# A written list of places for the weight splits of an encoder trunk, in place of a model of time

## The chip, the core and the metric

The kernel runs on one core of a Trainium2 chip. Its engines are TensorE (PE in the profile: matmuls, with PEld for its weight loads), VectorE (DVE), ScalarE (ACT), GpSimd (POOL) and SyncE (SP, which here only issues DMAs). Each has a queue of its own and works through it in order; between queues, semaphores hold an instruction back until what it needs is there. The metric is the time of one execution on the device in microseconds (us), as the median of several runs.

## The reference

The program is an encoder of two layers over a sequence of 256 tokens of width 1024, in float32. Each layer is a feed-forward block (SwiGLU), a mixer, and a second feed-forward block, each with a residual and a layer norm behind it. The mixer of the first layer is a bidirectional chunkwise mLSTM, that of the second a windowed attention with grouped heads.

```python
for l in range(DEPTH):
    x = layer_norm(ALPHA * x + 0.5 * swiglu(x, ffn_w_in[l, 0], ffn_w_out[l, 0]), ln_g[l, 0], ln_b[l, 0])
    j = l // N_MIXERS
    if l % N_MIXERS == 0:
        y = mlstm_mixer(x, ml_w_in[j], ml_gate_b[j], ml_norm_g[j], ml_w_out[j])
    else:
        y = window_attention(x, at_w_in[j], at_sink[j], at_w_out[j])
    x = layer_norm(ALPHA * x + y, ln_g[l, 1], ln_b[l, 1])
    x = layer_norm(ALPHA * x + 0.5 * swiglu(x, ffn_w_in[l, 1], ffn_w_out[l, 1]), ln_g[l, 2], ln_b[l, 2])

def swiglu(x, w_in, w_out):
    gu = x @ w_in
    g, u = gu[..., :D_FF], gu[..., D_FF:]
    return (jax.nn.silu(g) * u) @ w_out
```

With D_FF = 2816 the four feed-forward blocks hold nearly all of the weights and of the multiplications.

## The kernel before, in words

**Tiles and stages.** All 256 tokens stay on the chip: x as two tiles of 128 tokens, its transpose xT, and the hidden h. The weights stream through. There are six stages in a row, two FFN blocks around the mLSTM, then two around the attention. An FFN stage has two wide units of 512 columns and then three groups; a group is a unit of 256 columns (`beside`) and one of 512 (`seven`), the latter with seven products of half-size blocks in place of eight, for which sums of weight blocks are built beforehand. The second weight matrix is multiplied in as soon as its part of h is there (`down`), and six last rows of it in `tail`, with the layer norm (`Norm`) behind.

**Splits.** Every float32 factor is cut in two parts whose sum it is, a rounded one (`_hi`, float32r) and the rest (`_lo`), and every product is three matmuls (`mm3`: hi by hi, hi by lo, lo by hi). For a piece of weights, 128 by 1024, `Weights.high` writes w_hi on ACT, `Weights.low` writes w_lo on DVE. There are 388 pieces, in the order in which PE uses them (the plan). Weight sums for `seven` are done by `Weights.sum`, either on DVE (s_raw added to s_raw, 72 of them) or by an accumulating DMA issued on POOL (24). The same two engines also move every PSUM result out and split it (`split_evac`: h_hi and h_lo, xT_hi and xT_lo, ...), compute the activations, the products of gate and value, and the layer norms.

**Buffers and loads.** Raw weights are loaded into 4 buffers (w_raw), inside an FFN stage also into 6 (s_raw) and 2 more (v_raw). When the last split or sum of a raw tile is placed, `drop` frees it and `load` puts the next DMA on SP's queue; it waits there for the semaphores of the freed buffer. Split parts live in a ring of 10 pairs; `done` tells that PE has been given its last use of a pair, and raises `room`, up to which the splits may go ahead.

**What sets the order.** The order of instructions on each queue is the order in which the program calls them. For all but splits and sums it is written out in the stages. Splits and sums are slipped in between them:

- Inside an FFN stage by a model of time (`Paced`, L48): while the program is written, it adds up for each engine when an instruction would end (`on_vector`, `on_scalar`, `on_tensor`), marks for each tile when it would be there, and after every matmul calls `fill` (L266), which places a split or a sum when its engine would otherwise be no more than 300 ns ahead of PE.
- In the mixers and at the seams by counts: every `W.done(upto, most)` (L295) places up to so many splits there, the counts in lists written by hand (PU, TD, MP, PD at L29 to L36).
- `take` calls `split`, which places whatever the next pieces still lack.

Every engine call goes through `Engine.call` in L134, so that most instructions of the profile stand at that line, and are told apart by their tiles. An accumulating sum is issued at L263, loads at L98 and L100, the layer norm's g and b at L517.

Of the kernel before, what the change touches and what calls it, by code (L numbers as in the profile page):

```python
# [1 line left out]

# [26 lines left out]
PU = [3, 1, 2, 1, 1, 1, 1, 1, 0, 1, 1, 2]  # L29
# [4 lines left out]
TD = [0, 3, 2, 0, 2, 2]  # L34
MP = [1, 0, 0, 0, 1, 0, 1, 1, 0, 0, 0, 0, 2, 2, 2]
PD = [8, 0, 5, 9, 6]  # L36
# [3 lines left out]
AHEAD = 300.0  # L40
SOON = -1000.0
LANDING = 2200.0
LOADING = 1340.0
SECOND = 1250.0
ADDING = 8000.0


class Paced:  # L48

    def __init__(self, nc):
        self.nc = nc
        self.pe = self.vec = self.act = self.dma = 0.0
        self.there, self.places = {}, {}
        self.filler, self.alone = None, True
        self.vector = Engine(nc.vector, self.on_vector)
        self.scalar = Engine(nc.scalar, self.on_scalar)
        self.tensor = Engine(nc.tensor, self.on_tensor)
# [3 lines left out]

    def place(self, ap):

        f = ap.ap[0][0]
        key = (ap.offset % f if f else 0, tuple(ap.ap[1:]))
        if key not in self.places:
            i = np.array([key[0]])
            for step, n in key[1]:  # L70
                i = (i[:, None] + step * np.arange(n if step else 1)[None, :]).reshape(-1)
            self.places[key] = i
        return self.places[key]

    def when(self, *aps):
        t = 0.0
        for ap in aps:
            a = self.there.get(ap.name)
            if a is not None:
                i = self.place(ap)  # L80
                t = max(t, a[i[i < a.size]].max(initial=0.0))
        return t

    def mark(self, ap, t):
        i = self.place(ap)
        a = self.there.get(ap.name)
        if a is None or a.size <= i.max():
            self.there[ap.name] = np.zeros(int(i.max()) + 1)
            if a is not None:
                self.there[ap.name][:a.size] = a  # L90
        self.there[ap.name][i] = t

    def load(self, ap, source, engine=None):
        if engine is not None:
            engine.dma_start(ap, source)
        elif isinstance(source, list):
            for k, src in enumerate(source):
                self.nc.sync.dma_start(ap[:, k].rearrange("p (m f) -> p m f", m=src.shape[1]), src)  # L98
        else:
            self.nc.sync.dma_start(ap, source)  # L100
        come = self.pe + LANDING
        alone, self.alone = self.alone, come > self.dma
        self.dma = max(self.dma, come) + LOADING + (SECOND if alone and not self.alone else 0.0)
        self.mark(ap, self.dma)

    def on_vector(self, name, n, out, ins):
        self.vec = max(self.vec, self.when(*ins)) + (n + 71) / 0.96
        for o in out:
            self.mark(o, self.vec + 115)

    def on_scalar(self, name, n, out, ins):
        self.act = max(self.act, self.when(*ins)) + n * 0.912 + 25
        for o in out:
            self.mark(o, self.act + 125)

    def on_tensor(self, name, n, out, ins):
        self.pe = max(self.pe, self.when(*ins)) + (109.0 if name == "transpose" else n / 2.4 + 13.3)
        for o in out:
            self.mark(o, self.pe + 200)
        if self.filler is not None:  # L120
            self.filler()


class Engine:
    def __init__(self, engine, told):
        self.engine, self.told = engine, told

    def __getattr__(self, name):
        f = getattr(self.engine, name)
        if name.startswith("preload"):  # L130
            return f

        def call(out, *args, **kw):
            r = f(out, *args, **kw)  # L134
            ins = [x for x in [*args, *kw.values()] if hasattr(x, "ap")]
            outs = [out] + ([kw["accum_out"]] if "accum_out" in kw else [])
            size = lambda x: int(np.prod(x.shape[1:]))
            self.told(name, size(out) if name in ("matmul", "transpose") else max(map(size, [out] + ins)), outs, ins)
            return r
        return call  # L140


class Weights:
# [5 lines left out]
    def __init__(self, nc, pool, words, plan, after):  # L149
        self.nc, self.pool, self.words, self.plan, self.after = nc, pool, words, plan, after  # L150
        self.raw, self.parts, self.half, self.sums = {}, {}, [], []
# [4 lines left out]
        self.uses = [0] * len(words)  # L156
        for p in plan:
            self.uses[p["word"]] += 1
# [45 lines left out]
    def split(self, upto):  # L204
        while self.made < min(upto, len(self.plan)):
            self.high()
        while self.half and self.half[0][0] < upto:
            self.low()

    def high(self):  # L210

        nc, i = self.nc, self.made
        p = self.plan[i]
        while self.half and (p["word"] not in self.raw or any(h[0] == p["needs"] for h in self.half)):
            self.low()
        while any(s_[0] == p["needs"] or p["word"] not in self.raw for s_ in self.sums):
            self.sum()
        if p["word"] not in self.raw:
            return False
# [12 lines left out]
        return True  # L232

    def low(self):

        nc = self.nc
# [13 lines left out]
        self.sums += [(i, *sum_) for sum_ in self.after.get(i, ())]  # L250
# [3 lines left out]
    def sum(self):  # L254
        nc = self.nc
        _, w, v = self.sums.pop(0)
# [5 lines left out]
        else:  # L262
            nc.gpsimd.dma_start(t.rearrange("p (k f) -> p k f", k=self.words[w]["k"]), v, accum_op=OP.add)  # L263
            nc.mark(t, max(nc.vec, nc.pe) + ADDING)

    def fill(self):  # L266

        nc = self.nc
        while True:
            act, vec = max(nc.act, nc.pe), max(nc.vec, nc.pe)  # L270
            if act < nc.pe + AHEAD and len(self.half) < 2 and self.made < min(self.room, len(self.plan)):
                p = self.plan[self.made]
                if (p["word"] in self.raw and nc.when(self.raw[p["word"]]) < act + SOON
                        and not any(p["needs"] == x for x in [h[0] for h in self.half] + [s_[0] for s_ in self.sums])):
                    self.high()
                    continue
            if vec < nc.pe + AHEAD:
                if self.half and nc.when(self.half[0][1]) < vec + SOON:
                    self.low()
                    continue  # L280
                if self.sums and nc.when(*(self.raw[w] for w in self.sums[0][1:] if isinstance(w, int))) < vec + SOON:
                    self.sum()
                    continue
            break

    def take(self, n):
        i = self.used
        self.used += n
        self.split(self.used)
# [5 lines left out]
    def done(self, upto=None, most=None, high_only=False):  # L295

# [1065 lines left out]
```

## Time and profile before

| what | value |
|---|---|
| median of 3 runs | 942.11 us |
| lowest and highest | 941.06 and 942.29 us |
| span of the profiled execution | 941.2 us |
| PE busy | 925.3 us, 98% of the span, 4416 matmuls |
| DVE busy | 800.0 us, 85%, 943 instructions |
| ACT busy | 546.5 us, 58%, 781 |
| POOL busy | 103.2 us, 11%, 162 |
| from HBM | 185.68 MB, 198 GB/s over the span |

The span is that of one execution taken with the profiler, from its first instruction to its last; that execution was not one of the three that were timed, and of its time only the span is given. A row of the profile names line, engine, operation, the tile written and the tiles read (`w_lo<-w_raw,w_hi`); in the order of time a row has start and duration in us, and in brackets how long the engine had been idle before it and what ended that wait. A row "x2" holds two such instructions in a run.

### The profile page before, as it was taken

Reading aid. Unit: us, or ns where it says so; the run is one execution under the profiler, and the core shown is the slowest. Engines: PE = TensorE matmul, PEld = TensorE weight load, DVE = VectorE, ACT = ScalarE, POOL = GpSimd, SP = SyncE. Lnnn points to the kernel's source line nnn. Section 1 sums busy time; section 2 is a strip of 40 time slices with the busy share of each in tenths; the row PEclk is TensorE's granted clock in tenths of the full one; section 3 lists DMA queues with packets and bytes.
Section 4 is the critical chain, followed back from the end, with each engine's and each line's share of the span. In section 5 each row is a group of like instructions: output and inputs, shape, how many; then the busy total and the mean of one; then the engine's idle time right before and its main releaser. Section 6 shows DMA issues by size and latency. Waiting matters only on the chain.

```text
span 941.2 us, 12338 instructions
## 1 busy us (share of the span) xinstructions
PE 925.3 (98%) x4416; PEld 766.4 (81%) x4416; DVE 800.0 (85%) x943; ACT 546.5 (58%) x781; POOL 103.2 (11%) x162
## 2 busy tenths in 40 slices
PE   9999999999999999999999999999999999999996
PEld 7788888889878787888888888887887788888885
DVE  6899997787697889988888899977878888898975
ACT  5656756347563548565535566563678554757460
POOL 0030101011111000101010101010544300000100
PEclk9999999999999999999999999999999999999999
DMA  7969773646534949685549597746543266769531
GB/s 267 358 154 338 209 265 75 216 134 204 177 108 145 314 150 327 173 327 134 180 155 338 132 324 210 249 90 200 175 147 104 68 215 254 229 219 306 162 91 45
DMA packets 98461, 187.54 MB, mean 199 GB/s; under 512 B 6720, under 2 KB 37456, under 8 KB 98400
## 3 DMA queue, kind: packets, MB, share of 16 engines
q1 hardware_dynamic: 91072, 173.04, 53.1%
q0 software_dynamic: 6752, 12.66, 8.4%
q10 hardware_dynamic: 576, 1.05, 0.3%
q8 instruction: 35, 0.57, 0.2%
q14 instruction: 26, 0.21, 0.1%
HBM read 185.68 MB, written 1.05 MB: 198 GB/s over the span
## 4 chain that ended last, share of the span: by engine, by line
PE 73%; DVE 12%; DMA 6%; ACT 4%; issue 3%; POOL 1%; SPq 0%; DVEq 0%; ACTq 0%
PE pw L134 46%; PE py L134 27%; DVE w_lo L134 5%; DMA w_raw<-in_ffn_w_in_dram 3%; ACT w_hi L134 2%; DMA w_raw<-in_ffn_w_out_dram 1%; DVE s_raw L134 1%; DMA s_raw<-in_ffn_w_in_dram 1%; ACT sc L134 1%; DVE h L134 1%; DVE o L134 1%; DVE e L134 1%; DMA w_raw<-in_ml_w_in_dram 0%; DVE pr_lo L134 0%; ACT xT_hi L134 0%
## 5 line engine op out<-in xcount | busy, mean ns | idle before, releaser
L134 DVE TENSOR_TENSOR w_lo<-w_raw,w_hi 128x1024 fp32r<-128x1024 f32 (+1 forms) x237 | 280.9, 1216 | 16.0 <-ACT w_hi L134 14.0
L134 ACT CAST w_hi<-w_raw 128x1024 fp32r<-128x1024 f32 (+1 forms) x237 | 240.4, 1049 | 75.4 <-DMA w_raw<-in_ffn_w_out_dram 21.7
L134 PE MATMUL pw<-w_hi,xT_hi 128*128 128x512 f32 x560 | 222.6, 397 | 0.2 <-ACT xT_hi L134 0.2
L134 PE MATMUL pw<-w_hi,xT_lo 128*128 128x512 f32 x560 | 218.9, 391 | 0.2 <-DVE xT_lo L134 0.2
L134 PE MATMUL pw<-w_lo,xT_hi 128*128 128x512 f32 x560 | 218.3, 390 | 0.2 <-DVE w_lo L134 0.2
L134 ACT CAST w_hi<-s_raw 128x1024 fp32r<-128x1024 f32 x144 | 148.4, 1052 | 94.1 <-DVE s_raw L134 58.3
L134 DVE TENSOR_TENSOR w_lo<-s_raw,w_hi 128x1024 fp32r<-128x1024 f32 x144 | 172.6, 1219 | 19.2 <-ACT w_hi L134 19.1
L134 PE MATMUL py<-w_hi,h_hi 128*128 128x512 f32 x352 | 138.2, 393 | 0.3 <-ACT h_hi L134 0.3
L134 PE MATMUL py<-w_hi,h_lo 128*128 128x512 f32 x352 | 137.4, 390 | 0.2 <-DVE h_lo L134 0.2
L134 PE MATMUL py<-w_lo,h_hi 128*128 128x512 f32 x352 | 137.1, 390 | 0.2 <-DVE w_lo L134 0.2
L134 PEld LDWEIGHTS pw<-w_hi,xT_lo 128*128 128x128 f32 x560 | 105.1, 188 | 23.7 <-DVE xT_lo L134 1.0
L134 PEld LDWEIGHTS pw<-w_lo,xT_hi 128*128 128x128 f32 x560 | 105.4, 188 | 21.3 <-DVE w_lo L134 0.9
L134 PEld LDWEIGHTS pw<-w_hi,xT_hi 128*128 128x128 f32 x560 | 105.3, 188 | 21.0 <-ACT xT_hi L134 1.0
L134 DVE TENSOR_TENSOR s_raw<-s_raw 128x1024 f32<-128x1024 f32 x72 | 87.0, 1219 | 0.6
L263 POOL DMA_DIRECT2D s_raw<-in_ffn_w_in_dram x24 | 29.2, 1215 | 496.9 <-DVE w_lo L134 378.7
L134 PEld LDWEIGHTS py<-w_hi,h_lo 128*128 128x128 f32 x352 | 66.1, 188 | 15.2 <-DVE h_lo L134 1.4
L134 PEld LDWEIGHTS py<-w_lo,h_hi 128*128 128x128 f32 x352 | 66.1, 188 | 13.9 <-DVE w_lo L134 0.6
L134 PEld LDWEIGHTS py<-w_hi,h_hi 128*128 128x128 f32 x352 | 66.1, 188 | 13.9 <-ACT h_hi L134 0.7
L134 PE MATMUL pw<-w_hi,S_hi 128*128 128x512 f32 x192 | 74.7, 389 | 0.0
L134 PE MATMUL pw<-w_hi,S_lo 128*128 128x512 f32 x192 | 74.7, 389 | 0.0
L134 PE MATMUL pw<-w_lo,S_hi 128*128 128x512 f32 x192 | 74.7, 389 | 0.0
L134 DVE TENSOR_TENSOR h_lo<-pw,h_hi 128x512 fp32r<-128x512 f32 x44 | 30.1, 687 | 24.5 <-ACT h_hi L134 24.4
(218 smaller groups left out, 1118.1 us busy)
## 6 DMA issues: line engine op xcount, KB each, us to landing
w_raw<-in_ffn_w_out_dram SPq DMA_DIRECT2D x88, 512.0 KB, 5.3
s_raw<-in_ffn_w_in_dram SPq DMA_DIRECT2D x72, 512.0 KB, 6.1
w_raw<-in_ffn_w_in_dram SPq DMA_DIRECT2D x56, 512.0 KB, 5.2
w_raw<-in_ffn_w_in_dram SPq DMA_DIRECT2D x96, 256.0 KB, 4.7
s_raw<-in_ffn_w_in_dram POOLq DMA_DIRECT2D x24, 512.0 KB, 6.1
w_raw<-in_ml_w_in_dram SPq DMA_DIRECT2D x24, 512.0 KB, 4.6
w_raw<-in_at_w_in_dram SPq DMA_DIRECT2D x12, 512.0 KB, 3.8
w_raw<-in_ml_w_out_dram SPq DMA_DIRECT2D x8, 512.0 KB, 3.8
```

Source lines behind the costliest of these rows:

```text
L134: r = f(out, *args, **kw)
L263: nc.gpsimd.dma_start(t.rearrange("p (k f) -> p k f", k=self.words[w]["k"]), v, accum_op=OP.add)
```

## The change

The model of time goes: `Paced` with its marks and its three clocks, `fill`, `lows`, and the constants for it. The hand-written counts PU, TD, MP and PD go too, as does `W.split` at the start. In their place stands `ORDER`, a string of letters and steps: H is a w_hi, L a w_lo, S a sum on DVE, A a sum by DMA. Each step is a number of instructions to be counted on from the entry before. `Counted` counts every compute instruction of the four engines (DMAs, table loads, splits and sums themselves aside) and after each calls `W.run`, which places every entry whose count has come and whose inputs are at hand (`ready`), the earliest in the list first. What PE is about to take (`upto`) is still forced out. `done` only frees parts and raises `room`. Sums on DVE and sums by DMA become two lists, so that one does not hold up the other.

The two programs have the same instructions. Leaving out splits, sums and weight loads, each engine has them in the same order, but for the pairs of ln_g and ln_b loads on SP, which stand one or two weight loads away from where they stood. The w_hi among themselves, the w_lo and the sums keep their order as well; what differs is behind which other instruction each of them stands.

```diff
-PU = [3, 1, 2, 1, 1, 1, 1, 1, 0, 1, 1, 2]
-TD = [0, 3, 2, 0, 2, 2]
-MP = [1, 0, 0, 0, 1, 0, 1, 1, 0, 0, 0, 0, 2, 2, 2]
-PD = [8, 0, 5, 9, 6]
-AHEAD = 300.0
-SOON = -1000.0
...
-class Paced:
...
+ORDER = (
+    "H19L0H16L0H33L3H2H5L1H6L2L3H1H4L1H0H1L8L2H29L6L1H1H19H10L7L5H7L0H1L2L0H6H15H3L2L0S1L0S0H1H29L3S1L4H5S0H3H6L7S3"
...
+class Counted:
+    def __init__(self, nc):
+        self.nc, self.n, self.then = nc, 0, None
+        for name in ("tensor", "vector", "scalar", "gpsimd"):
+            setattr(self, name, Engine(self, getattr(nc, name)))
...
 class Engine:
...
+        f, c = getattr(self.engine, name), self.counted
+        if name.startswith("preload") or "dma" in name:
             return f
+        def call(*args, **kw):
+            r = f(*args, **kw)
+            c.n += 1
+            if c.then is not None:
+                c.then()
             return r
...
+    def ready(self, what):
+        if what == "L":
+            return bool(self.half)
+        if what in self.sums:
+            q = self.sums[what]
+            return bool(q) and all(w in self.raw for w in q[0][1:] if isinstance(w, int)) and not any(
+                x[0] == q[0][0] for x in (self.sums["S"] if what == "A" else ()))
+        p = self.plan[self.made] if self.made < min(self.room, len(self.plan)) else None
+        return p is not None and p["word"] in self.raw and not any(
+            x[0] == p["needs"] and (len(x) == 2 or x[1] == p["word"])
+            for x in self.half + self.sums["S"] + self.sums["A"])
+
+    def run(self, upto=0):
+        while True:
+            early = self.made < upto or self.half and self.half[0][0] < upto
+            next_ = [(o[0], what) for what, o in self.order.items()
+                     if o and (early or o[0][0] <= self.nc.n) and self.ready(what)]
+            if not next_:
+                assert not early, (self.made, self.used, self.nc.n)
+                break
+            _, what = min(next_)
+            self.order[what].pop(0)
+            self.high() if what == "H" else self.low() if what == "L" else self.sum(what)
...
-    def fill(self):
-        nc = self.nc
-        while True:
-            act, vec = max(nc.act, nc.pe), max(nc.vec, nc.pe)
-            if act < nc.pe + AHEAD and len(self.half) < 2 and self.made < min(self.room, len(self.plan)):
...
     def take(self, n):
         i = self.used
         self.used += n
-        self.split(self.used)
+        self.run(self.used)
...
-    def done(self, upto=None, most=None, high_only=False):
+    def done(self, upto=None):
...
-        if self.nc.filler is not None:
-            self.fill()
-            return
-        end = min(self.room if most is None else min(self.room, self.made + most), len(self.plan))
-        while self.made < end and self.high():
-            pass
-        if not high_only:
-            self.lows()
+        self.run()
...
+    W.room = RING
+    nc.then = W.run
...
-        W.done(most=TD[bound[0]])
+        W.done()
...
-        nc.filler = W.fill if kind == "ffn" else None
```

More of the change, by code (lines that the diff above doesn't have):

```diff
@@ L202, in drop @@
             self.free[self.words[w]["in"]] += 1
[L204 to L208, printed above, removed]
+    def ready(self, what):
[20 more added lines that the diff above has]
+            self.high() if what == "H" else self.low() if what == "L" else self.sum(what)
     def high(self):
[L212 removed]
+        nc, i = self.nc.nc, self.made
         p = self.plan[i]
[L214 to L219, printed above, removed]
         scale, raw = p["scale"], self.raw[p["word"]]
```

167 lines of the change are left out of this document (42 added, 125 removed).

## The prediction

> **What bounds the kernel now.** I read the page first, then the waits of PE's weight loads, then busy time by stretches, then the order of time at each wait. From the page:
>
> ```profile
> span 941.2 us, 12338 instructions
> PE 925.3 (98%) x4416; PEld 766.4 (81%) x4416; DVE 800.0 (85%) x943; ACT 546.5 (58%) x781; POOL 103.2 (11%) x162
> PEclk9999999999999999999999999999999999999999
> ```
>
> TensorE is busy for 98% of the span at the full granted clock. The pace of its work is in the chain of waits, the stretches behind it in the busy time by windows:
>
> ```profile
> 804.76 5.44 PE pw L134 x24
> ...
> 103.00:150.00 47.00, 47.00 (x214) 38.89 (x214) 42.74 (x43) 29.50 (x37) 3.60 (x3) 1.00 0.80 244
> 127.00:150.00 23.00, 23.00 (x107) 19.05 (x106) 20.01 (x20) 11.61 (x16) 2.39 (x2) 1.00 0.56 150
> ```
>
> The first row is 24 matmuls in 5.44 us, 0.227 us each, with nothing waited for. The second (columns: us, PE, PEld, DVE, ACT, POOL busy, clock, DMA share, GB/s) is a group in the first FFN: PE busy for all 47 us, so whatever DVE (42.74) and ACT (29.50) do there in another order returns nothing. A list of places can only return time where PE stands still. Those places are in the waits of its weight loads (wait in total, times, longest); here are the first and the last of 17 rows, which sum to 22.0 us in 41 waits, with one that I use between:
>
> ```profile
> PEld pw L134 <- DVE pr_lo L134: 3.7, 9, 0.7
> ...
> PEld py L134 <- DVE w_lo L134: 1.7, 3, 0.7
> ...
> PEld py L134 <- DVE q_lo L134: 0.2, 1, 0.2
> ```
>
> A wait costs PE less than its row says, since a weight load normally runs ahead of a matmul that is still streaming. At the end of the second layer's first FFN (ACT, PE and weight-load rows in the order of time):
>
> ```profile
> 642.11 1.05 ACT L134 CAST w_hi<-w_raw 128x1024 fp32r<-128x1024 f32 x1
> 643.00 0.40 PE L134 MATMUL py<-w_hi,h_lo 128*128 128x512 f32 x1
> 643.05 0.58 ACT L134 CAST h_hi<-pw 128x512 fp32r<-128x512 f32 x1
> ...
> 643.68 0.19 PEld L134 LDWEIGHTS py<-w_hi,h_hi 128*128 128x128 f32 x1 [0.72 <-ACT h_hi L134]
> 644.41 0.19 PEld L134 LDWEIGHTS py<-w_hi,h_lo 128*128 128x128 f32 x1 [0.43 <-DVE h_lo L134]
> ...
> 644.75 0.39 PE L134 MATMUL py<-w_hi,h_hi 128*128 128x512 f32 x1
> ```
>
> Four matmuls start between 643.00 and 644.75: 1.75 us for 0.91 us of work, so 0.84 us lost where the two waits read 0.72 + 0.43 = 1.15. I take 0.15 us off each wait. All 41 are then worth 22.0 - 41 x 0.15 = 15.9 us, of which some 2 lie before the first weights arrive. About 14 us is the most that any order could return.
>
> **The change part by part.** Both programs hold the same instructions with the same operands, and on PE, and on ACT, DVE and POOL leaving the splits and sums out, in the same order. The model of time runs while the program is written, so taking it out costs the chip nothing. What changes is how many splits (w_hi on ACT, w_lo on DVE, numbered here along their engine) and sums stand ahead of each other instruction: a different number for 208 of 360 instructions on ACT and 248 of 482 on DVE, mostly by one or two, up to seven. A split takes its engine about 0.95 us (ACT) or 1.14 us (DVE), so each place is one such step times what PE waits for there. On SP, four pairs of ln_g and ln_b loads go ahead of one or two weight loads, a fifth goes behind one, and a few weight loads change places or buffers with a neighbour. The first weight load so passed shows the cover:
>
> ```profile
> 170.32 0.37 SPq L100 DMA_DIRECT2D w_raw<-in_ml_w_in_dram  x1
> ...
> 187.56 2.01 ACT L134 CAST w_hi<-w_raw 128x1024 fp32r<-128x1024 f32 x2
> ```
>
> It is issued 17 us before its w_hi reads it and would be held up by two loads; without that cover each of the two would cost its share of a load. Nothing, then. POOL keeps its order. Place by place, from the large to the small:
>
> (1) 643 us, above. Before, ACT runs w_hi 287 at 642.11 and only then h_hi. The list puts w_hi 287 and 288 behind both h_hi of that place, and three w_lo fewer stand ahead of h_lo on DVE. h_hi can start 0.94 us earlier: all 0.84 us returns.
>
> (2) 312 us, the same kind:
>
> ```profile
> 310.85 1.05 ACT L134 CAST w_hi<-w_raw 128x1024 fp32r<-128x1024 f32 x1 [1.05 <-DMA w_raw<-in_ffn_w_in_dram]
> 312.43 0.19 PEld L134 LDWEIGHTS pw<-w_hi,xT_hi 128*128 128x128 f32 x1 [0.60 <-ACT xT_hi L134]
> ...
> 313.16 0.19 PEld L134 LDWEIGHTS pw<-w_hi,xT_lo 128*128 128x128 f32 x1 [0.43 <-DVE xT_lo L134]
> ```
>
> One w_hi fewer stands ahead of xT_hi (and one w_lo fewer ahead of xT_lo), so it no longer waits out the w_hi at 310.85, which itself waited 1.05 us for a load. 0.60 + 0.43 - 0.30 = 0.73 us returns.
>
> (3) 464 us. Two w_lo run back to back just ahead of the instructions PE wants:
>
> ```profile
> 461.36 2.35 DVE L134 TENSOR_TENSOR w_lo<-w_raw,w_hi 128x1024 fp32r<-128x1024 f32 x2
> ...
> 464.97 0.19 PEld L134 LDWEIGHTS py<-w_hi,h_lo 128*128 128x128 f32 x1 [0.67 <-DVE h_lo L134]
> ```
>
> The list leaves one of them there: 1.14 us earlier, 0.67 - 0.15 = 0.52 us returns.
>
> (4) 250 to 282 us, the end of the mLSTM:
>
> ```profile
> 250.67 0.88 DVE L134 SCALAR_TENSOR_TENSOR h<-py,den,h 128x256 f32<-128x256 f32 x2 [0.61 <-ACT h L134]
> 250.88 1.15 ACT L134 ACTIVATE w_hi<-w_raw,gcol 128x1024 fp32r<-128x1024 f32 x1
> ...
> 252.07 1.28 DVE L134 SCALAR_TENSOR_TENSOR w_lo<-w_raw,gcol,w_hi 128x1024 fp32r<-128x1024 f32 x1 [0.53 <-ACT w_hi L134]
> 253.27 1.01 DVE L134 TENSOR_TENSOR wt<-pw,wt 128x512 f32<-128x512 f32 x2
> ...
> 258.46 0.19 PEld L134 LDWEIGHTS py<-v_hi,a_hi 128*128 128x128 f32 x1 [0.68 <-ACT h L134]
> ...
> 264.43 0.19 PEld L134 LDWEIGHTS py<-v_hi,a_hi 128*128 128x128 f32 x1 [1.18 <-ACT h L134]
> ...
> 280.38 0.19 PEld L134 LDWEIGHTS py<-w_lo,xT_hi 128*128 128x128 f32 x1 [0.44 <-DVE w_lo L134]
> ...
> 281.57 0.19 PEld L134 LDWEIGHTS py<-w_lo,xT_hi 128*128 128x128 f32 x1 [0.67 <-DVE w_lo L134]
> ```
>
> Four waits, 2.97 - 0.60 = 2.37 us. One w_hi leaves the place at 250.88, and its w_lo no longer stands at 252.07 ahead of wt but ahead of the h at 250.67, where DVE idles for 0.61 us. So the 0.53 us of idle and the 1.20 us to wt go, and 1.20 - 0.61 = 0.59 us comes: DVE's chain of wt, den and h, which ACT's h and then PE follow, starts 1.14 us earlier. From there to 281 DVE is one chain, and PE gains no more than the chain does. I take 1.1 us; what is left of the four waits stays.
>
> (5) 200 us. Two w_lo move from ahead of DVE's last layer-norm steps (192 to 196.5 us) to behind them, and the transposes that follow come earlier:
>
> ```profile
> 200.38 0.19 PEld L134 LDWEIGHTS pw<-xT_lo,gw_hi 128*128 128x128 f32 x1 [0.40 <-DVE xT_lo L134]
> ```
>
> The wait goes: 0.25 us.
>
> (6) 687 to 707 us, attention. One w_hi more stands ahead of the first exponentials, and POOL's scaling follows them; one w_lo and one w_hi fewer ahead of the next turn:
>
> ```profile
> 687.39 2.95 ACT L134 CAST w_hi<-w_raw 128x1024 fp32r<-128x1024 f32 x3
> 690.53 0.47 ACT L134 ACTIVATE sc<-pw,nm 128x256 f32<-128x256 f32 x1 [0.20 <-DVE nm L134]
> ...
> 698.05 0.14 PEld L134 LDWEIGHTS pw<-ident,sc 128*128 128x128 f32 x1 [0.70 <-POOL sc L1229]
> ...
> 706.47 0.42 PEld L134 LDWEIGHTS pw<-ident,sc 128*128 128x128 f32 x4 [1.15 <-ACT pr_hi L134]
> ```
>
> 0.95 less the 0.20 us that sc waits anyway is 0.75 us lost at 698; at 706 PE comes that much later and the 1.15 - 0.15 = 1.00 us there goes: 0.25, or about 0.2 us, returns in all. The other heads keep their order and their waits (3.7 us for pr_lo).
>
> Returned: 0.84 + 0.73 + 0.52 + 1.10 + 0.25 + 0.20 = 3.64 us.
>
> What it costs is where the list puts splits later. The clearest place is 124 us: six w_hi and six w_lo that stood ahead of h_hi and h_lo now stand behind. They are 6 x 1.14 = 6.8 us of DVE work, pushed into the stretch from 127 to 150 where DVE has 23.00 - 20.01 = 2.99 us to spare; the hh behind it was done 5.2 us before PE used it. 6.8 - 2.99 - 5.2 is below zero, so it fits, with 1.4 us in hand. But a split also frees the buffer of a load, so loads go out later too:
>
> ```profile
> w_raw<-in_ffn_w_out_dram SPq DMA_DIRECT2D x88, 512.0 KB, 5.3
> ...
> w_raw<-in_ml_w_out_dram SPq DMA_DIRECT2D x1, 512.0 KB, 3.3
> ...
> 32.16 10.70 DMA w_raw<-in_ffn_w_in_dram
> ...
> 38.42 0.19 PEld L134 LDWEIGHTS pw<-w_lo,xT_hi 128*128 128x128 f32 x1 [0.56 <-DVE w_lo L134]
> ...
> 63.86 0.19 PEld L134 LDWEIGHTS py<-w_lo,h_hi 128*128 128x128 f32 x1 [0.59 <-DVE w_lo L134]
> ```
>
> A load takes 5.3 us in the median, 3.3 us alone (the row of the one issued at 253 us), 10.70 in the rush at the start. With 3.3 the 1.4 us hold and nothing is lost; with 5.3 the excess of 2.0 us breaks them by 0.6. I count four such places: 36 to 64 us, where the loads come at their latest and three w_lo go ahead of an h_lo (0 to 1.2 us, less the two waits at 38 and 64, 1.15 - 0.30 = 0.85, that may go), 147 us (0 to 1.5), 492 us (0 to 0.5), 913 us (0 to 1.3). Low ends are likelier, since the loads that go later are no longer in a rush: 0.15 us each, 0.6 us in all. The Trainium skill ("DMA: Bandwidth & Descriptors", Anatomy of one DMA) fits a DMA's time as 2.0 us and its bytes over 436 GB/s, measured on GpSimd's path; for 512 KB that is an estimated 3.2 us, as the lone load agrees and the median does not, and by it these places cost nothing and the time would be 0.6 us lower.
>
> The sum: 941.2 - 3.64 + 0.6 = 938.2 us of span. The median of the runs, 942.11, lies 0.9 us above this span, so 939.1 us.
>
> **The rivals.** *The waits come back.* PE ahead of time meets the next late instruction: (4) is such a chain, and FFN groups with DVE at 42.74 of 47 have little room. For it: four waits in a row in (4); against it: (1), (2) and (3) are followed by stretches in which PE waits for nothing. If half of the 3.64 returns and the four places cost 0.6, 940.9 us, no change that can be told (a run of this kernel can tell about 0.2%, 1.9 us).
>
> *Late splits starve PE: slower.* Its place is the end of every FFN group, twelve in all, where w_lo wait for loads that left late. At 0.6 us a group (the excess above) 7.2 us are lost, 942.1 - 3.64 + 7.2 = 945.7 us. It decides from (3.64 + 1.9) / 12 = 0.46 us a group. Against it: PE waits for a w_lo in three rows of 1.7 us now, and only the group at 124 moves by as many as six.
>
> *The list does not move what PE waits for.* Then 942 us. The order says otherwise at six places.
>
> **How the numbers follow.** Forecast 939.1 us, 0.62; waits come back or nothing moves, 0.27; late splits, 0.11. Best case: all 3.64, no cost, the two early waits (0.85) and 2 us more of attention's 3.7 us for pr_lo: 935.6. Worst: half returns and the four places cost their full 4.5 us: 942.1 - 1.8 + 4.5 = 944.8, of which I keep 944.0. Range 935.5 to 944.0. Faster by over 0.2% 0.62, within 0.27, slower 0.11.
>
> **What would show it.** Right: no wait of PE's weight loads for h_hi near 643, xT_hi near 312, h_lo near 464; DVE's wt near 252; a longer wait for POOL's sc near 698. Wrong: PE's weight loads waiting for hh or h_lo near 45, 147 or 913, and ACT's w_hi waiting longer for DMA than now.

## The result: 0.33% faster, and the profile after

| | before | changed |
|---|---|---|
| median of 6 runs each, us | 941.65 (941.06 to 942.29) | 938.44 (936.88 to 940.00) |
| ratio, 95% interval | | 0.9967 [0.9955, 0.9978] |
| span of the profiled execution, us | 941.2 | 936.9 |

3.2 us less, where 939.1 us was forecast. The profiled executions differ by 4.3 us, so about 1 us of their difference is chance; the table below shows where it sits. The page of the changed kernel, its first line and the line of busy time:

```profile
span 936.9 us, 12306 instructions
PE 921.7 (98%) x4416; PEld 766.2 (82%) x4416; DVE 796.1 (85%) x943; ACT 542.4 (58%) x781; POOL 102.5 (11%) x162
```

PE's busy time fell by 3.6 us with the same 4416 matmuls, so that row holds some of the waiting too. The waits of its weight loads (in total, times, longest), three of 16 rows:

```profile
PEld pw L91 <- DVE pr_lo L91: 3.3, 8, 0.7
PEld py L91 <- DVE h_lo L91: 2.7, 5, 2.0
PEld pw L91 <- DVE e L91: 1.5, 1, 1.5
```

All 16 rows sum to 17.6 us in 31 waits, against 22.0 us in 41 before. Two waits are new and long: one of 2.0 us for h_lo and one of 1.5 us for e. At place (1), in the order of time:

```profile
639.19 0.58 ACT L91 CAST h_hi<-pw 128x512 fp32r<-128x512 f32 x1
...
640.67 0.19 PEld L91 LDWEIGHTS py<-w_hi,h_lo 128*128 128x128 f32 x1 [0.17 <-DVE h_lo L91]
```

h_hi no longer stands behind a w_hi, and of 0.72 + 0.43 us of waits 0.17 is left.

PE runs the same 4416 matmuls in the same order in both kernels, so the starts of the same two matmuls in two traces give how much sooner (minus) or later (plus) PE got through the stretch between them. The next column is the same for two other executions: the changed program with the places of before in its list (told below), and the changed kernel run again. The last column compares before with that list of its own places: one order of ACT, DVE, POOL and PE, two executions.

| stretch, us of before | PE waits for | forecast | before to changed | the same, other executions | same order twice |
|---|---|---|---|---|---|
| 1-24 | x, first weights | none | -0.39 | +1.17 | -0.18 |
| 24-42 | hh, w_lo | 0, may go | -0.79 | +0.41 | -0.79 |
| 42-49 | h_lo | +0.15 (0 to 1.2) | **+1.89** | **+1.43** | 0.00 |
| 55-69 | w_lo | 0, may go | -0.41 | -0.17 | -0.25 |
| 144-157 | hh | +0.15 (0 to 1.5) | +0.21 | +0.47 | -0.03 |
| 196-203, (5) | xT_lo | -0.25 | -0.37 | -0.36 | -0.01 |
| 256-285, (4) | h, w_lo | -1.10 | -1.39 | -1.42 | -0.01 |
| 308-317, (2) | xT_hi, xT_lo | -0.73 | -0.74 | -0.79 | +0.05 |
| 323-332 | hh | none | +0.21 | +0.07 | -0.12 |
| 363-368 | e | none | **-0.81** | **-0.96** | +0.13 |
| 461-468, (3) | h_lo | -0.52 | -0.52 | -0.51 | -0.03 |
| 491-496 | xT_lo | +0.15 (0 to 0.5) | +0.19 | -0.04 | -0.01 |
| 641-646, (1) | h_hi, h_lo | -0.84 | -0.83 | -0.82 | -0.01 |
| 684-714, (6) | sc, pr_hi, pr_lo | -0.20 | **-1.48** | **-1.42** | 0.00 |
| 765-771 | xT_hi, xT_lo | none | -0.71 | -0.03 | -0.67 |
| 910-915 | e | +0.15 (0 to 1.3) | **+1.36** | **+1.21** | 0.00 |
| all the rest | | none | +0.22 | +0.21 | -0.06 |
| span | | -3.0 | -4.36 | -1.55 | -1.99 |

The rows fall in two kinds. At 42, 196, 256, 308, 363, 461, 641, 684 and 910 us the step comes again within 0.15 us (0.46 at 42), and two executions of one order agree within 0.13: here the order decides. At the start, 24, 55, 144 and 765 us two executions differ by as much as the two kernels do: there PE waits for what hangs on the landing of a load, and a single trace tells nothing. By the first kind alone the list returns 6.14 us and costs 3.25.

The larger loss, 40 to 46 us of the changed kernel:

```profile
39.84 1.05 ACT L201 CAST w_hi<-w_raw 128x1024 fp32r<-128x1024 f32 x1 [4.31 <-DMA w_raw<-in_ffn_w_out_dram]
...
40.80 0.58 ACT L91 CAST h_hi<-pw 128x512 fp32r<-128x512 f32 x1
...
41.41 0.69 DVE L91 TENSOR_TENSOR h_lo<-pw,h_hi 128x512 fp32r<-128x512 f32 x1 [2.64 <-ACT h_hi L91]
...
43.15 2.35 DVE L219 TENSOR_TENSOR w_lo<-s_raw,w_hi 128x1024 fp32r<-128x1024 f32 x2
43.18 0.58 ACT L91 CAST h_hi<-pw 128x512 fp32r<-128x512 f32 x1
...
45.42 0.68 DVE L91 TENSOR_TENSOR h_lo<-pw,h_hi 128x512 fp32r<-128x512 f32 x1
...
46.16 0.19 PEld L91 LDWEIGHTS py<-w_hi,h_lo 128*128 128x128 f32 x1 [2.02 <-DVE h_lo L91]
```

Read from the end: PE waits for the second h_lo, which stands behind three w_lo on DVE; but DVE had stood idle for 2.64 us before, since the first h_hi stood on ACT behind a w_hi that waited 4.31 us for its load. Before, both h_hi stood ahead of that w_hi (ACT of before):

```profile
37.38 1.18 ACT L134 CAST h_hi<-pw 128x512 fp32r<-128x512 f32 x2 [1.11 <-PE pw L134]
40.25 1.05 ACT L134 CAST w_hi<-w_raw 128x1024 fp32r<-128x1024 f32 x1 [1.69 <-DMA w_raw<-in_ffn_w_out_dram]
```

The other loss begins 40 us ahead of the place where PE shows it:

```profile
869.20 1.05 ACT L201 CAST w_hi<-w_raw 128x1024 fp32r<-128x1024 f32 x1 [5.26 <-DMA w_raw<-in_ffn_w_out_dram]
...
872.05 0.58 ACT L91 ACTIVATE g<-pw 128x512 f32<-128x512 f32 x1
...
872.67 0.69 DVE L91 TENSOR_TENSOR e<-g,e 128x512 f32<-128x512 f32 x1 [2.71 <-ACT g L91]
...
903.72 4.62 DVE L219 TENSOR_TENSOR w_lo<-w_raw,w_hi 128x1024 fp32r<-128x1024 f32 x4
908.26 0.68 DVE L91 TENSOR_TENSOR e<-e,pw 128x512 f32<-128x512 f32 x1
...
909.00 0.19 PEld L91 LDWEIGHTS pw<-w_hi,xT_hi 128*128 128x128 f32 x1 [1.47 <-DVE e L91]
```

Here the list did not put the w_hi ahead of g: before, it already stood ahead of both h_hi and g. ACT of before, then the load of this w_hi on SP, of before and of the changed kernel:

```profile
868.02 1.05 ACT L134 CAST w_hi<-w_raw 128x1024 fp32r<-128x1024 f32 x1 [2.23 <-DMA w_raw<-in_ffn_w_out_dram]
...
869.92 0.57 ACT L134 CAST h_hi<-pw 128x512 fp32r<-128x512 f32 x1
872.00 0.60 ACT L134 ACTIVATE g<-pw 128x512 f32<-128x512 f32 x1 [1.50 <-PE pw L134]
```
```profile
862.46 0.34 SPq L100 DMA_DIRECT2D w_raw<-in_ffn_w_out_dram  x1
```
```profile
863.70 0.34 SPq L78 DMA_DIRECT2D w_raw<-in_ffn_w_out_dram  x1
```

The load goes out 1.24 us later in a kernel whose PE is 5.98 us ahead by then, so 7.2 us later as PE sees it: 0.71 us ahead of a certain matmul before, 6.51 us behind the same one in the changed kernel. In both kernels its issue waits for the same w_lo on DVE, which frees the buffer.

### The profile page after: what moved, and what is told of

Same layout as the page of the kernel before. It is cut to its first block, busy times and chain, and to the rows that moved or that the text cites. A ratio compares the mean times of both kernels' runs of the same rounds, so it can differ in the third digit from the quotient of the medians.

```text
span 936.9 us, 12306 instructions
## 1 busy us (share of the span) xinstructions
PE 921.7 (98%) x4416; PEld 766.2 (82%) x4416; DVE 796.1 (85%) x943; ACT 542.4 (58%) x781; POOL 102.5 (11%) x162
## 4 chain that ended last, share of the span: by engine, by line
PE 85%; DVE 6%; DMA 3%; ACT 3%; issue 2%; SPq 1%; POOL 0%; DVEq 0%; ACTq 0%
PE pw L91 54%; PE py L91 31%; DVE w_lo L219 2%; DMA w_raw<-in_ffn_w_out_dram 2%; ACT w_hi L201 1%; DMA w_raw<-in_ffn_w_in_dram 1%; ACT sc L91 1%; SPq L78 1%; DVE rm L91 1%; DVE o L91 0%; DVE x L91 0%; ACT o L91 0%; DMA x<-in_x_dram 0%; SPq L76 0%; POOL sc L91 0%
## 5 line engine op out<-in xcount | busy, mean ns | idle before, releaser
L219 DVE TENSOR_TENSOR w_lo<-w_raw,w_hi 128x1024 fp32r<-128x1024 f32 x235 | 280.5, 1221 | 10.5 <-ACT w_hi L201 9.7
L201 ACT CAST w_hi<-w_raw 128x1024 fp32r<-128x1024 f32 x235 | 238.4, 1052 | 68.9 <-DMA w_raw<-in_ffn_w_in_dram 25.7
L91 ACT CAST h_hi<-pw 128x512 fp32r<-128x512 f32 x44 | 25.7, 584 | 66.3 <-PE pw L91 66.3
```

Of the source, the lines that this page charges most:

```text
L91: r = f(*args, **kw)
L201: nc.scalar.copy(hi, raw)
L219: nc.vector.tensor_sub(lo, raw, hi.bitcast(F32))
```

## The experiments

All kernels are the changed one with other steps in ORDER; most diffs show the order that results on the engine, with w_hi and w_lo numbered along it. A ratio is always to runs of before beside them on the same chip, and a range in brackets its 95% interval.

### Before's places, written as a list

```diff
 ORDER = (
-    "H19L0H16L0H33L3H2H5L1H6L2L3H1H4L1H0H1L8L2...
+    "H19L0H16L0H33L3H2L4H1L5H2L5H1L5H5H7L11H0L5...
```

> The changed program with another list: every split and sum stands behind the instruction behind which the model of time had put it, so ACT, DVE, POOL and PE run exactly the order of before; on SP one pair of ln_g and ln_b loads stands two weight loads later, and twice two weight loads go ahead of such a pair. If the gain is the places alone, as I hold: the time of before, 941.65 us within 0.5. The rival, that part of the gain comes from what goes with the new program whatever its list says: at or below 940.5 us.

941.69 us beside 942.61 of before, 0.9991 [0.9981, 1.0000]. The middle is 0.9 us below before and the interval ends at it, so the times alone don't exclude a small part from elsewhere. The last column of the table, which comes from this run, does not show one: where the order decides, the two executions agree within 0.13 us. So the places are the gain, as far as these runs can tell.

### Three places alone

```diff
 312 us, ACT
-w_hi 124, w_hi 125, sg, w_hi 126, xT_hi, xT_hi
+w_hi 124, sg, w_hi 125, xT_hi, xT_hi, w_hi 126
...
```

and in the same way two w_lo there, five w_hi and eight w_lo at 464 us, four and six at 643 us.

> The order of before, with the list's places only at 312 us (two w_hi, two w_lo), 464 us (five w_hi, eight w_lo) and 643 us (four w_hi, six w_lo). My theory, that each of these waits is removed by itself and PE keeps what it gains: the three waits of 0.73, 0.52 and 0.84 us go, 941.65 - 2.09 = 939.6 us. The rival, that waits come back further on (PE ahead of time meets the next late instruction): half of it, 940.6 us or more, with a new or longer wait behind 312, 464 or 643 in the trace.

942.15 us, 0.9997 [0.9986, 1.0007]: no gain. In the trace all three stretches return what was forecast (-0.74, -0.54, -0.82 us), and 323 to 332 us costs +2.09. (363 to 368 us returns 0.80 as well, of which more below.) ACT, DVE and PE's weight loads there, in the order of time:

```profile
327.23 1.05 ACT L200 CAST w_hi<-s_raw 128x1024 fp32r<-128x1024 f32 x1 [1.72 <-DMA s_raw<-in_ffn_w_in_dram]
328.18 0.62 ACT L90 CAST S_hi<-S 128x512 fp32r<-128x512 f32 x1
...
328.83 0.69 DVE L90 TENSOR_TENSOR S_lo<-S,S_hi 128x512 fp32r<-128x512 f32 x1 [3.93 <-ACT S_hi L90]
...
332.15 0.42 PEld L90 LDWEIGHTS pw<-ident,hh 128*128 128x128 f32 x4 [2.50 <-DVE hh L90]
```

Two w_hi wait for loads ahead of S_hi, DVE stands 3.93 us for S_hi, and PE 2.50 us for hh: the same pattern as at 40 us. Some 0.7 us more goes near 670 us, where the list's order runs back into that of before. So the theory of independent places falls: each returns its own part, but not without its surroundings.

### The three places with the rest of their group

```diff
 ACT, 319 to 331 us
-w_hi 130, sg, h_hi, w_hi 131, w_hi 132, S_hi, S_hi, w_hi 133
+sg, h_hi, S_hi, w_hi 130, w_hi 131, w_hi 132, S_hi, w_hi 133
```

and so on for eleven w_hi, ten w_lo and two sums up to 345 us.

> The kernel with the list's places at 312, 464 and 643 us alone, to which the rest of the list's places in the group that begins at 312 us are added (eleven w_hi, ten w_lo and two sums up to 345 us). With the three alone PE lost 1.96 us for hh at 330 us, where two w_hi that waited for their loads stood ahead of S_hi on ACT. My theory: places hang together within a group, since a split placed later frees its buffer later; with the list's order S_hi stands ahead of the late w_hi, the 1.96 us become 0.4 or less, and the time is 2.0 us below before, ratio 0.998. The rival, that the loss at 330 us was chance in the loads: it is gone in this run too, but then DVE's wait for S_hi is short because no w_hi waits for a load there, not because S_hi stands ahead of it; or it stays, above 1 us.

940.77 us beside 941.94, 0.9981 [0.9972, 0.9991]. The stretch 323 to 332 us returns 0.20 us in place of costing 2.09, and the gain of the three places is there. DVE and ACT in the order of time: S_hi runs ahead of the three w_hi, and S_lo follows at once. The last of these w_hi ends at 326.72 us, so behind them S_hi would have come 4 us later; that the loads came sooner here (waits of 0.72 and 0.29 us in place of 2.02 and 1.72) is thus not what saved it. A w_hi that waits 3.33 us for its load, behind both S_hi as in the run before, holds up nobody:

```profile
322.67 0.69 DVE L90 TENSOR_TENSOR S_lo<-S,S_hi 128x512 fp32r<-128x512 f32 x1 [0.69 <-ACT S_hi L90]
...
325.66 1.06 ACT L200 CAST w_hi<-s_raw 128x1024 fp32r<-128x1024 f32 x1 [0.29 <-DMA s_raw<-in_ffn_w_in_dram]
...
330.57 1.05 ACT L200 CAST w_hi<-w_raw 128x1024 fp32r<-128x1024 f32 x1 [3.33 <-DMA w_raw<-in_ffn_w_in_dram]
```

### At 44 us: three w_lo behind h_lo

```diff
 ORDER
-7L0H1L2L0H6
+7H1L4L0L0H4
 DVE
-h_lo, w_lo 14, w_lo 15, w_lo 16, h_lo
+h_lo, h_lo, w_lo 14, w_lo 15, w_lo 16
```

> The changed kernel with one step undone: at 44 us three w_lo go behind h_lo (the second of its pair) on DVE, nothing else moves. There PE stands 1.75 us for h_lo. If the three w_lo in front of it are the cause: h_lo runs as soon as its h_hi is there (43.76 us), PE's wait shrinks to 0.1 to 0.3 us, and the time is 938.44 - 1.5 = 936.9 us. If the cause is ACT, where a w_hi that waits 4.31 us for its load stands ahead of both h_hi: the wait stays above 1 us, and the time within 0.6 of 938.4.

941.41 us, 0.9990 [0.9982, 0.9999], slower than the changed kernel's 0.9967, which neither theory foresaw. PE's wait for h_lo is gone, and PE stands for hh instead. DVE, and then PE's weight loads, in the order of time:

```profile
43.25 0.69 DVE L91 TENSOR_TENSOR h_lo<-pw,h_hi 128x512 fp32r<-128x512 f32 x1 [1.95 <-ACT h_hi L91]
45.63 0.69 DVE L91 TENSOR_TENSOR h_lo<-pw,h_hi 128x512 fp32r<-128x512 f32 x1 [1.69 <-ACT h_hi L91]
```
```profile
55.78 0.53 PEld L91 LDWEIGHTS pw<-ident,hh 128*128 128x128 f32 x4 [2.85 <-DVE hh L91]
```

DVE now idles twice for h_hi (1.95 and 1.69 us) and has all its w_lo still to do. What was in short supply is DVE's time up to hh; the three w_lo only decided at which matmul PE noticed.

### At 40 us: w_hi behind both h_hi, w_lo behind both h_lo

```diff
 ACT
-w_hi 14, h_hi, w_hi 15, w_hi 16, h_hi
+h_hi, h_hi, w_hi 14, w_hi 15, w_hi 16
 DVE
-h_lo, w_lo 14, w_lo 15, w_lo 16, h_lo
+h_lo, h_lo, w_lo 14, w_lo 15, w_lo 16
```

> The changed kernel with the step at 40 us undone in full: three w_hi, the first of which waited 4.31 us for its load, go behind both h_hi on ACT, and their three w_lo behind both h_lo on DVE. My theory by now: not the three w_lo were the cause but the late load ahead of h_hi, since DVE lost 2.64 us there waiting for h_hi. Then DVE waits under 1 us for h_hi, PE waits under 0.4 us for h_lo, and for hh 7 us later (2.85 us when the three w_lo alone were moved) no longer than 0.5; 1.5 to 1.9 us faster than the changed kernel. The rival, that DVE simply has more to do up to hh than PE leaves time for: a wait of 1 us or more for hh stays, and the time within 0.6 us of the changed kernel.

937.51 us beside 942.50, 0.9945 [0.9926, 0.9963]; the changed kernel beside it took 938.99. ACT, and then PE's weight loads, in the order of time:

```profile
37.03 1.16 ACT L91 CAST h_hi<-pw 128x512 fp32r<-128x512 f32 x2 [1.15 <-PE pw L91]
...
40.88 1.05 ACT L201 CAST w_hi<-w_raw 128x1024 fp32r<-128x1024 f32 x1 [2.69 <-DMA w_raw<-in_ffn_w_out_dram]
```
```profile
51.52 0.53 PEld L91 LDWEIGHTS pw<-ident,hh 128*128 128x128 f32 x4 [0.76 <-DVE hh L91]
```

PE no longer waits for h_lo near 44 us. For hh it waits 0.76 us, not the 0.5 at most that was expected: here w_hi 14 waited 2.69 us for its load, and w_lo 14 after it 1.65 us. In the next run, where the load came earlier (1.50 us), there is no such wait. So the late load ahead of h_hi was the cause: moving the three w_lo alone only shifted the loss, and moving the w_hi with them took away DVE's wait for h_hi. What remains hangs on the load itself. The times alone would not settle this, since the intervals of this run and of the changed kernel overlap.

### At 869 us: three w_hi behind g

```diff
 ACT
-h_hi, w_hi 366, w_hi 367, w_hi 368, g
+h_hi, g, w_hi 366, w_hi 367, w_hi 368
```

> The changed kernel with one step undone 40 us ahead of where PE loses time: on ACT three w_hi at 869 us, the first of which waits 5.26 us for its load, go behind g, nothing else moves. My theory: the late g cost DVE 2.71 us of idle time at 870 us, DVE has nothing to spare from there on, and that is why PE stands 1.2 us for e at 908 us. Then DVE's e runs near 870.0 instead of 872.7, PE's wait at 908 falls below 0.4 us, and the time is 938.44 - 1.2 = 937.2 us. The rival, that the eight w_lo in a row ahead of that e on DVE (899 to 908 us) are enough by themselves, or that the loads set their pace: the wait stays at 1 us or more, and the time within 0.4 of 938.4.

938.01 us beside 942.61, 0.9958 [0.9944, 0.9971]. ACT, and then PE's weight loads, in the order of time:

```profile
867.73 0.60 ACT L91 ACTIVATE g<-pw 128x512 f32<-128x512 f32 x1 [2.17 <-PE pw L91]
870.21 1.05 ACT L201 CAST w_hi<-w_raw 128x1024 fp32r<-128x1024 f32 x1 [1.87 <-DMA w_raw<-in_ffn_w_out_dram]
```
```profile
909.19 0.19 PEld L91 LDWEIGHTS pw<-w_hi,xT_hi 128*128 128x128 f32 x1 [0.15 <-DVE e L91]
```

DVE's e runs without an idle time ahead of it (at 871.49 us, in an execution in which PE was 1.6 us later by then), and 38 us later PE's wait is 0.15 us in place of 1.47, though the eight w_lo ahead of the second e stand where they stood. The load still goes out 6.51 us behind the same matmul, so here the late load by itself cost nothing; its price comes from what stands behind it. The stretch 910 to 915 us returns 1.17 us against the changed kernel run again. The interval of the time alone would not settle it; the row does.

### Both places mended, and the changed kernel beside it

> The changed kernel with both steps undone, at 40 us as in the run before and at 869 us (three w_hi behind g). If the two places are independent, as PE's full busy time between them says: 1.7 + 1.2 = 2.9 us below the changed kernel, some 935.5 us where that takes 938.4, ratio to before 0.9935. If what is gained at 40 us is lost again on the way: 937 us, the gain of the second place alone.

> The changed kernel as it is, beside the other runs on the same chip: ratio to before 0.996 to 0.998. PE's waits that a queue's order sets come again within 0.2 us (h_lo at 44 us 1.7 to 2.2, e at 908 us 1.0 to 1.6, sc at 699 us 0.6 to 0.9); if the two large ones are chance, one of them is under 0.5 here.

The changed kernel again: 938.99 us beside 942.50, 0.9960 [0.9947, 0.9972], with waits of 1.6 us for h_lo, 1.3 for e and 0.8 for sc: not chance. Both places mended: 936.08 us (935.24 to 937.62), 0.9934 [0.9916, 0.9952]; in the trace 42 to 49 us returns 1.43 and 910 to 915 us 1.17 us. 936.08 beats the changed kernel by 2.9 us, as expected, and each place returns in this trace what it returned in the run that mended it alone: the two are independent of each other.

### The attention: one w_lo away from POOL

```diff
 DVE
-pr_lo, pr_lo, w_lo 302, q_lo, ... pr_lo, q_lo, pr_lo, w_lo 303
+pr_lo, pr_lo, q_lo, ... pr_lo, q_lo, pr_lo, w_lo 302, w_lo 303
```

> The changed kernel with one w_lo of the attention, at 698 us on DVE, moved 6.5 us later (behind the second pr_lo of the next turn, next to the w_lo that stands there). A POOL instruction that starts while DVE runs a w_lo (both inputs in SBUF) seems to end only behind that w_lo: sc, four times, took 2.80 us with it and 1.85 without. If that is so: these four take 1.85 to 1.9 us, and PE's wait of 0.8 us for sc at 699 falls under 0.2; DVE is a w_lo later from 706 us, so a wait for pr_lo or sc behind it may grow by up to 0.9 us. The rival, that POOL's time has another cause (its own first instruction, a DMA): the four still take 2.6 us or more.

In the one execution of this kernel POOL's four sc took 1.85 us, and PE's wait of 0.8 us for them is gone. It came back: PE lost 0.53 us at the sc of the next turn, 0.2 at the pr_lo behind it and 0.76 at the turn after, where POOL's sm, begun next to two w_lo, took 1.88 in place of 1.02 us. The run as a whole (941.03 us) also met a drop of TensorE's clock, told at the end.

### The attention: six w_lo one turn later, and four w_hi behind pr_hi

On top of both places mended, w_lo 302 to 307 each one turn later; then also four w_hi:

```diff
 ACT, four turns
-pr_hi, w_hi, q_hi, pr_hi
+pr_hi, q_hi, pr_hi, w_hi
```

> The kernel with both places mended, and in the attention six w_lo on DVE each moved one turn later (698 to 731 us; they are done 27 to 35 us before PE uses them): the turn at 698 has none, the others one as before, the last goes where DVE idles. If POOL is held by the w_lo next to it: sc of the second turn takes 1.85 us for four in place of 2.8, PE's wait of 0.7 us for sc goes and, with no turn that has two w_lo, does not come back; 0.7 us less than with both places mended, ratio to before 0.9927. The rival, that the turns are a chain of ACT and DVE in which PE only waits elsewhere: the wait moves to the next pr_lo or sc and the ratio stays at 0.9934.

> As the run before, and on ACT four w_hi of the attention (700, 719, 725 us and the one at 713) go from between the two pr_hi of their turn to behind the second. If the w_hi in between is what makes pr_lo late: PE's waits for pr_lo (3.3 us in 8) fall by 0.8 us or more, ratio 0.9919. The rival: the w_hi then stands ahead of the four sc of the next turn on ACT, and what is gained at pr_lo is lost at sc or nm; the sum of the waits in the attention stays within 0.3 us of the run before, or grows.

936.76 us beside 941.94, 0.9949 [0.9936, 0.9961], and 937.85 us, 0.9961 [0.9949, 0.9974]: the waits moved, as both rivals said, and neither kernel is faster than the one with both places mended. With the w_lo later PE gains 0.73 us at 698, loses 0.72 in the next turn, and 1.04 in the last one (0.3 of it comes back behind it), where the last w_lo, put into a gap of DVE, met POOL. POOL and DVE of the first of the two runs:

```profile
731.39 3.06 POOL L91 TENSOR_SCALAR sc<-sc,sm 128x256 f32<-128x256 f32 x4
```
```profile
732.97 1.21 DVE L219 TENSOR_TENSOR w_lo<-w_raw,w_hi 128x1024 fp32r<-128x1024 f32 x1
```

With the w_hi later too, PE's waits from 675 to 745 us read:

```profile
PEld pw L91 <- DVE pr_lo L91: 3.4, 7, 0.9
PEld pw L91 <- ACT pr_hi L91: 2.4, 4, 0.9
```

pr_lo is not shorter, and pr_hi, 0.5 us in the run without it, is 2.4: a w_hi behind pr_hi holds up the four sc of the next turn, and these the pr_hi that follow.

### The last of the six away from POOL

```diff
 DVE
-pr_lo, pr_lo, q_lo, w_lo 307, o, o, pr_lo, pr_lo, q_lo
+pr_lo, pr_lo, q_lo, o, o, pr_lo, pr_lo, q_lo, w_lo 307
```

> The run with six w_lo one turn later, and the last of them (733.0 us, next to POOL's sc of the last turn, which took 3.06 us for four) moved 4 us on, to a gap in which POOL has nothing to do. If a w_lo next to POOL is what cost 1.07 us there: sc of the last turn takes 1.84 to 2.0 us, PE's wait of 1.2 us for it falls under 0.3, and the kernel is 1 us faster than with the w_lo at 733, level with the one that has both places mended only (ratio to before 0.993 to 0.9935), since the 0.73 us won at 698 came back as 0.65 in the two turns behind it. The rival, that the last turn is late by ACT and DVE's own chain: sc is short but PE waits for it as long as before.

936.35 us beside 942.76, 0.9931 [0.9918, 0.9945].

```profile
731.29 2.00 POOL L91 TENSOR_SCALAR sc<-sc,sm 128x256 f32<-128x256 f32 x4
```

These are POOL's last four sc. PE's wait of 1.2 us for them is gone, and PE gets past them 1.06 us sooner. This kernel and the one with both places mended are level (0.9931 and 0.9934) and faster than both kernels of this case.

## Why the prediction was right

The sum was: 3.64 us returned, 0.6 us of cost, 939.1 us. The time, 938.44, is close. But by the table 6.14 us were returned and 3.25 lost where the order decides: two errors of some 2.5 us each cancelled, and that they did is luck. The last step, 0.9 us from span to time, holds only as a difference: in every later run the time is 1.7 to 1.8 us above the span, so the profiled execution of before was itself some 1.3 us above its median, an estimate from its span of 941.2. Of the signs that were named, one of being right (a longer wait for sc near 698) did not come, and two of being wrong did, while the time still fell: a wait of 2.0 us for h_lo near 45, and w_hi waiting longer for DMA (54.7 us in all, 50.3 before). Point by point:

- **(1), (2), (3), 643, 312 and 464 us.** Forecast 0.84, 0.73 and 0.52, measured 0.83, 0.74 and 0.52. Reading a wait's row, taking 0.15 us off, and asking whether one split fewer stands ahead holds to 0.02 us for a wait with a single instruction in front. That PE would keep them without the rest of the list does not follow, as the run of three places showed.
- **(4), the end of the mLSTM.** 1.10 forecast, 1.39 measured. As argued, the w_lo moved into DVE's idle time ahead of h. The step "I take 1.1 us; what is left of the four waits stays" was a little too careful.
- **(5).** 0.25 forecast, 0.37 measured.
- **(6), attention.** The step that failed is "0.95 less the 0.20 us that sc waits anyway is 0.75 us lost at 698". The exponentials did come later, but the wait at 698 was not theirs, and in the changed kernel it is gone. In the profile of before, POOL and DVE:

```profile
692.91 1.00 POOL L1225 TENSOR_TENSOR sm<-sm,es 128x4 f32<-128x4 f32 x1 [10.38 <-ACT es L134]
...
695.12 2.88 POOL L1229 TENSOR_SCALAR sc<-sc,sm 128x256 f32<-128x256 f32 x4
```
```profile
696.44 1.21 DVE L134 TENSOR_TENSOR w_lo<-w_raw,w_hi 128x1024 fp32r<-128x1024 f32 x1
```

sm takes 0.20 us and four sc take 1.85 elsewhere; both were long because a w_lo ran next to them. In the changed kernel those w_lo stand elsewhere, POOL is 1.8 us shorter there, and one sc is long a turn later instead (POOL of the changed kernel):

```profile
691.23 1.85 POOL L91 TENSOR_SCALAR sc<-sc,sm 128x256 f32<-128x256 f32 x4
...
696.98 2.80 POOL L91 TENSOR_SCALAR sc<-sc,sm 128x256 f32<-128x256 f32 x4
```

  In all 1.48 us returned, not 0.20. The rows of 1.00 and 2.88 us stood in the profile of before; I read when POOL started and not how long it took.
- **A place I missed, 366 us.** It returned 0.81 us. In the waits it stands as "issue", which I left out. Before, two w_lo (363.10 to 365.37 us) stood ahead of the e that PE transposes next; the list leaves one. But that alone is not shown to be the cause: the two runs with the places at 312, 464 and 643 us, without and with their group, return 0.80 us here too, though both w_lo stand there as before and no order differs from that of before between 345 us and here. Without the group, PE had just lost 2.09 us and comes later; with it, DVE is 1.5 us further ahead of PE at this e, by what it no longer lost between 312 and 334 us. PE showed at 366 us what DVE had lost 30 to 50 us earlier. What the one w_lo fewer adds stays open. DVE of before, and PE's weight loads:

```profile
365.37 0.68 DVE L134 TENSOR_TENSOR e<-pw,e 128x512 f32<-128x512 f32 x1
366.09 0.69 DVE L134 TENSOR_TENSOR e<-e,e 128x512 f32<-128x512 f32 x1
```
```profile
366.90 0.42 PEld L134 LDWEIGHTS pw<-ident,e 128*128 128x128 f32 x4 [1.02 <-issue]
```

  and the same two w_lo, and no wait behind them, in the run with the whole group:

```profile
361.76 2.35 DVE L218 TENSOR_TENSOR w_lo<-s_raw,w_hi 128x1024 fp32r<-128x1024 f32 x2
```
```profile
366.07 0.59 PEld L90 LDWEIGHTS pw<-ident,e 128*128 128x128 f32 x4
```

- **The costs.** The four places were named, and two of them are the two losses; what failed is the size, "0.15 us each, 0.6 us in all", and its reason. 42 to 49 us cost 1.89 (1.43 in the other executions) against a bound of 1.2, and 910 us 1.36 (1.21) against 1.3; 147 and 492 us stay within chance. The cost was sized by the excess of a load's duration over the slack of DVE, and neither loss is that. At 40 us the w_hi that waits for its load starts about when it did (39.84 us, and 40.25 before); what moved is its place, to the front of h_hi; the three w_lo ahead of h_lo, which were named for this place, are not the cause, as the run that moved them alone shows. At 869 us the place ahead of g is the old one, and the load goes out 7.2 us later against PE. That loads leave later was thus right there; what they cost is not the excess but the time for which h_hi or g, and behind them DVE, stand still. Asking of each w_hi with a long wait for DMA what stands behind it on ACT points at both places. The median load from the second weight matrix took 5.5 us after and 5.3 before, and the cost hung on neither. So the estimated 3.2 us by the Trainium skill ("DMA: Bandwidth & Descriptors", Anatomy of one DMA), by which these places would have cost nothing, was no guide here.
- **The two early waits (38 and 64 us, 0.85 in the best case)** went in the trace, 0.79 and 0.41; but they also went with the places of before (0.79 and 0.25). That is chance in the loads, not the list.
- **The rivals.** "The waits come back" did not happen in the sum, but it is what happened in the runs with single steps: 2.09 of 2.10 us in that with three places, and in both runs of the attention. "Late splits starve PE" did not happen at every group's end; in two places PE did stand for what a late load had held up.

## What to carry to other kernels

An instruction that waits for a transfer costs nothing where nothing behind it is ready (3.33 us at 330 us in the run with the whole group), and much of its wait where something ready stands behind it (4.31 us at 40 us cost PE 1.4 to 1.9): look in the trace for long waits on DMA and ask what is next on that engine, and who stands idle for it. The price may show 40 us later, where an engine with nothing to spare runs out of lead; the place of the idle time, not that of PE's wait, is the one to mend. In the one group where both were tried, the places of the whole group returned what one place alone did not. And compare two traces of the same order first, to know at which places a single trace says something.

## What the runs showed of the hardware that I had not expected

**POOL stands behind DVE's w_lo.** A w_lo reads two tiles from SBUF. A POOL instruction that begins while one runs lasts until its end or up to 0.9 us longer: a single sc of 0.48 us became 1.44 us at 698 us in the changed kernel (twice), 0.48 when that w_lo was moved away. DVE's pr_lo and rm, which read PSUM, ran next to sc without an effect. The Trainium skill says so ("SBUF — State Buffer", Who interferes with whom: a VectorE instruction with two SBUF inputs contends with a GpSimd instruction that reads SBUF), and these runs agree. A gap on DVE is thus not free for a w_lo if POOL works then, as the 3.06 us above show (there the long sc began at 732.75 us, under a q_lo that reads two tiles from SBUF too, and the w_lo followed at 732.97).

**TensorE's clock was halved once behind a wait of 1.6 us.** In the run with one w_lo moved in the attention, PE stood 1.61 us idle at 44 us, as in the changed kernel (1.59 us). Busy time by windows (columns as in the prediction; the clock is third from the end):

```profile
47.00:48.00 1.00, 1.00 (x4) 0.71 (x3) 1.00 (x2) 0.00 (x0) 0.00 (x0) 0.50 0.09 25
```

and the same stretch of the changed kernel:

```profile
47.00:48.00 1.00, 1.00 (x6) 0.83 (x5) 1.00 (x2) 0.00 (x0) 0.00 (x0) 1.00 0.08 16
```

From 46.75 to 50.08 us matmuls start up to 0.43 us apart in place of 0.23, and 1.5 us are lost. It happened in one of four profiled executions with this wait (PE idle for 1.1 to 1.6 us). Two longer ones, 2.1 us at 330 us in the run of three places and 2.4 us at 53 us in the run with three w_lo moved, left the clock at full speed. The Trainium skill ("TensorE: Matmul & The Clock Gate", Why this matters for your kernels) advises against idle gaps of PE above some 3 us; here the drop came behind one of about half that. That the wait caused it is not shown, only that it followed 0.7 us after its end. It does not explain why the changed kernel's runs spread wider (936.88 to 940.00): the mean granted clock was 0.996 in the execution with the drop, and 0.998 or 0.999 in all six of these.
